# Even layer's value sums for two tiles of queries in one step, and the base weight block's copy moved from GpSimd to ScalarE

## The chip, the cores and the metric

The kernel runs on one NeuronCore of a Trainium2 chip. The metric is the device time of one execution in microseconds. The kernel before took 733.72 us (median of three runs, 733.67 to 733.96). The execution that the profiler recorded took 733.63 us; the span from its first to its last instruction is 731.9 us, so 1.7 us lie outside the span. All durations below come from that one execution.

## The reference

A two-layer encoder trunk on 256 tokens of width 1024, in float32. The even layer runs two kinds of attention side by side (8 heads of windowed two-dimensional attention with a bias, 8 heads of latent attention), the odd layer a mixture of three dilated windows. Each layer is followed by an MLP with a squared ReLU.

```python
for layer in range(DEPTH):                       # 2
    xn = rms_norm(x, norm_mix[layer])
    if layer % 2 == 0:
        x = x + even_mixer(xn, ...)              # softmax(q k^T + bias) v, two kinds
    else:
        x = x + odd_mixer(xn, ...)
    x = x + sq_relu_mlp(rms_norm(x, norm_mlp[layer]), mlp_w1[layer], mlp_w2[layer])
return rms_norm(x, norm_final)

def sq_relu_mlp(xn, w1, w2):                     # 1024 -> 4096 -> 1024
    return jnp.square(jax.nn.relu(xn @ w1)) @ w2
```

## The kernel before, in words

Every float32 weight is split on the chip into a high part (`whi`, a cast on ScalarE, line 205) and a low part (`wlo`, a subtraction on VectorE, line 206), and each product is three matmuls of these parts (`mm3`, lines 209 to 211). The whole weight set streams through the core once: `specs` lists the weight pieces in order of use, `load_weight` fetches a piece into one of four `raw` buffers by a DMA of the SyncE queue (line 151), `split_piece` splits it into one of three `whi`/`wlo` buffers, and `weight()` hands it to the matmuls, with loads four pieces ahead and splits two pieces ahead. So a cast waits until TensorE has let go of the piece three places back, and a load waits until the piece four places back has been split.

**Even layer.** `scores(n)` computes the scores and the softmax of one item (two heads, one tile of 128 queries), `turn_probs(n)` transposes the probabilities on TensorE (line 816) and copies them out, and `mix(n)` multiplies them with the values (four float32 matmuls, line 830, recorded as eight instructions) and splits the sum. There are 16 items. `attention()` lists these steps, and they are woven between the large projections.

**MLP.** Up pieces (U, from `w1`) and down pieces (D, from `w2`) alternate: U0 U1 U2 D0 U3 D1 and so on to D15. The down product uses seven block products in place of eight (`SEVEN`), for which sums of weight blocks are needed. For D0 to D13 of each MLP, `load_weight` does it in part by DMA: the base block goes into the first half of a `sum` buffer (three buffers; SyncE queue, line 143), **GpSimd copies it into the second half (line 144)**, and a DMA of GpSimd's queue adds two more blocks onto both halves while it writes (line 145). VectorE adds further blocks to that (`more_sums`, lines 179 and 180: these results go back into `raw` and into `every`), and `split_sums` splits the three sums into `sumh` (ScalarE) and `suml` (VectorE). Between these, the engines compute the hidden layer: ReLU and square on ScalarE (373, 375), three combinations on VectorE (380 to 382), their cast `hh` on ScalarE, and `hl` on VectorE.

Each engine executes its own instructions in the order that the program's scheduler has written; an instruction that waits holds up all behind it on that engine. The k-th line 179 needs what the k-th line 145 has added, and in VectorE's order it stands behind the splits of the sums before it (`suml`, `hl`) and ahead of the two low parts of the down piece before it.

Of the kernel before, what the change touches and what calls it, by code (L numbers as in the profile page):

```python
# [19 lines left out]
F32 = mybir.dt.float32  # L20
F32R = mybir.dt.float32r
AF = mybir.ActivationFunctionType
# [4 lines left out]
P = 128  # L27
D = 1024
KT = D // P
T = 256  # L30
NT = T // P
# [10 lines left out]
BLK = 512  # L42
LOAD_AHEAD = 4
# [6 lines left out]
def trunk(ctx, tc, a, out):  # L50
    nc = tc.nc
# [23 lines left out]
    def quarter_pair(name):  # L75
        return [act.tile([P, KT // 2, T], F32R, tag="quarter", name=name + v, bufs=4) for v in "hl"]

    def bank(tag):
        return ps.tile([P, 512], F32, tag=tag, name=tag)

    x = act.tile([P, KT, T], F32, name="x")
# [24 lines left out]
    specs = []  # L106
# [24 lines left out]
    plan_mlp(1)  # L131

    parts = {}
    state = {"loaded": 0, "split": (0, 0), "used": 0, "pool": None, "parts_done": None}

    def load_weight(pieces=1, before=lambda i: None):
        j = state["loaded"]
        src, n, _, seven = specs[j]
        if seven:

            blocks = src.rearrange("p (b n) -> p b n", n=BLK)
            sums = state["pool"].tile([P, 2, BLK], F32, tag="sum", name="sum", bufs=3)
            nc.sync.dma_start(sums[:, 0, :], blocks[:, 3, :])
            nc.gpsimd.tensor_copy(out=sums[:, 1, :], in_=sums[:, 0, :])  # L144
            nc.gpsimd.dma_start(sums, blocks[:, 0:3:2, :], accum_op=ALU.add)
            n = 3 * BLK
        raw = wraw.tile([P, WCH], F32, tag="raw", name="raw")
        for i in range(pieces):
            c = slice(i * n // pieces, (i + 1) * n // pieces)
            before(i)  # L150
            nc.sync.dma_start(raw[:, c], src[:, c])
        parts[j] = [raw, None, None] + ([sums] if seven else [])
        state["loaded"] = j + 1
# [5 lines left out]
    def split_piece(eng=None):  # L159
        j, i = state["split"]  # L160
        _, _, n, seven = specs[j]
        state["split"] = (j, i + 1) if i < n - (not seven) else (j + 1, 0)
        if i == 0:
            parts[j][1:3] = (wsp.tile([P, WCH], F32R, tag=v, name=v) for v in ("whi", "wlo"))
            if seven:

                with tc.issue_after(state["parts_done"]):
                    more_sums(parts[j])
        if i == n:
            parts[j][1:3] = split_sums(parts[j])  # L170
            return
        raw, hi, lo = (z[:, cut(j, i, n)] for z in parts[j][:3])
        return split(hi, lo, raw, eng)
# [16 lines left out]
    def prefetch(loads, splits):  # L190
        while state["loaded"] < min(loads, len(specs)):
            load_weight()
        while state["split"] < (min(splits, len(specs)), 0):
            split_piece()

    def weight():

        j = state["used"]
        prefetch(j + 1, j + 1)
        prefetch(j + LOAD_AHEAD, j + SPLIT_AHEAD)  # L200
        state["used"] = j + 1
        return parts.pop(j)[1:3]

    def split(hi, lo, src, eng=None):
        a = nc.scalar.copy(hi, src).ins  # L205
        return a, (eng or nc.vector).tensor_tensor(lo, src, hi.bitcast(F32), op=ALU.subtract).ins  # L206

    def mm3(o, sh, sl, mh, ml, first, last):
        nc.tensor.matmul(o, sh, mh, start=first, stop=False)  # L209
        nc.tensor.matmul(o, sh, ml, start=False, stop=False)  # L210
        nc.tensor.matmul(o, sl, mh, start=False, stop=last)  # L211

    def two_heads(o, hi, lo, ts):

        for n, (y, z) in enumerate(((hi, hi), (hi, lo), (lo, hi))):
            for j in range(2):
                pb = slice(64 * j, 64 * j + 64)
                nc.tensor.matmul(o[j], y[pb, 0, ts], z[pb, 1, :], start=n == 0, stop=n == 2)  # L218
# [10 lines left out]
    def tok(t):  # L229
        return slice(t * P, (t + 1) * P)  # L230
# [8 lines left out]
    def two(z):  # L239
        return z.rearrange("p (f n) -> p f n", f=2)  # L240
# [7 lines left out]
    def add_squares(b, s):  # L248

        q = scratch([2, T], "q") if b else two(s)  # L250
        nc.scalar.activation(q, x[:, 2 * b:2 * b + 2, :], AF.Square)
        if b:
            nc.vector.tensor_tensor(two(s), two(s), q, op=ALU.add)
        if b == 3:
            return nc.vector.tensor_tensor(s[:, 0:T], s[:, 0:T], s[:, T:2 * T], op=ALU.add).ins
# [308 lines left out]
    def even(ep):  # L564
# [208 lines left out]
        mixed = [quarter_pair("oa"), None]  # L773
        items = [(0, t, hp) for hp in range(4) for t in range(NT)] + [(1, t, hp) for hp in range(4) for t in range(NT)]
        biases, probs, turned = {}, {}, {}

        def load_bias(n):
            if n < 8:
                _, t, hp = items[n]
                biases[n] = ep.tile([P, 2, T], F32, tag="bias", name="bias", bufs=2)  # L780
                nc.sync.dma_start(biases[n], a["rpb"][t, hp])

        def scores(n):
            kind, t, hp = items[n]
            load_bias(n + 2)

            sb = [bank("w")[:, 0:T] for _ in range(2)] if kind == 0 else bank("w").rearrange("p (j n) -> p j n", j=2)
            s_of = lambda j: sb[j] if kind == 0 else sb[:, j]
            if kind == 0:
                two_heads(sb, *qk[hp], tok(t))  # L790
            else:
                for j in range(2):
                    h = 2 * hp + j
                    (qh, ql), (kh, kl) = mT["q"], mT["k"]
                    mm3(sb[:, j], qh[0:96, h, tok(t)], ql[0:96, h, tok(t)], kh[0:96, h, :], kl[0:96, h, :], True, True)
            pp, sn = scratch([2, T], "pp"), scratch([2, T], "sn")
            mn, z, rz = (work.tile([P, 2], F32, tag=v, name=v, bufs=3) for v in ("mn", "z", "rz"))
            for j in range(2):
                o = s_of(j)
                if kind == 0:  # L800
                    nc.vector.tensor_tensor_reduce(out=sn[:, j], in0=o, in1=biases[n][:, j, :], op0=ALU.add, op1=ALU.min,
                                                   scale=-1.0, scalar=3e38, accum_out=mn[:, j:j + 1])
                else:
                    nc.vector.tensor_scalar(sn[:, j], o, -MLA_SCALE, None, ALU.mult, ALU.min, accum_out=mn[:, j:j + 1])
            for j in range(2):
                nc.scalar.activation(pp[:, j], sn[:, j], AF.Exp, bias=mn[:, j:j + 1], scale=-1.0, accum_out=z[:, j:j + 1])
            nc.vector.reciprocal(rz, z)
            for j in range(2):
                nc.scalar.activation(pp[:, j], pp[:, j], AF.Copy, scale=rz[:, j:j + 1])
            probs[n] = pp  # L810
# [7 lines left out]
            nc.any.tensor_copy(out=turned[n], in_=pt.rearrange("p (b n) -> p b n", b=4))  # L818

        def mix(n):  # L820
            kind, t, hp = items[n]
            pts = turned.pop(n)
            if mixed[kind] is None:
                mixed[kind] = quarter_pair("ob")
            v = (vna, vml)[kind]
            pvo = bank("acc" if n < 6 else "w")
            for kk in range(NT):
                for j in range(2):
                    h = 2 * hp + j
                    nc.tensor.matmul(pvo[64 * j:64 * j + 64, 0:P], v[:, kk, h * 64:(h + 1) * 64], pts[:, 2 * j + kk, :],  # L830
                                     start=kk == 0, stop=kk == NT - 1)
            split(*(z[:, hp, tok(t)] for z in mixed[kind]), pvo[:, 0:P])

        def attention():

            out = []
            for n in range(len(items) + 2):
                for fn, m in ((scores, n), (turn_probs, n - 1), (mix, n - 2)):
                    if 0 <= m < len(items):
                        out.append(lambda fn=fn, m=m: fn(m))  # L840
                if n == 0:
                    out += [lambda: None] * 2
            return out
# [21 lines left out]
        main += [(0, lambda: accs.extend(open_accs()))]  # L865
        main += [(1.3, f) for k in range(6) for f in out_steps(accs, mixed, wo, k)]
        side = attention()
        at = -5
        total = sum(c for c, _ in main) + at
# [296 lines left out]
```

## Time and profile before

| what | value |
|---|---|
| profiled execution | 733.63 us |
| its span | 731.9 us |
| busy: VectorE, ScalarE, GpSimd | 623.0, 522.6, 78.8 us |
| granted TensorE clock, mean | 0.998 |
| even layer with its norm, from the first score matmul to the first MLP's norm sums | 39 to 133 us |
| first MLP: down pieces D0 to D13 | from 133 us, one down and one up piece every 10.54 us |
| second MLP: down pieces from D0 | from 570 us |

Rows of the timeline read: start in us, duration in us, engine, line, operation, result from operands, shape, count; in brackets the idle time of the engine before it and what ended it. Durations of neighbours on one engine overlap a little, so the cost of an instruction to its engine is the distance from its start to the next one's. PE is TensorE, PEld its weight loads, DVE VectorE, ACT ScalarE, POOL GpSimd, SPq the SyncE queue.

### The profile page before, as it was taken

Reading aid. Unit: us, or ns where it says so; the run is one execution under the profiler, and the core shown is the slowest. Engines: PE = TensorE matmul, PEld = TensorE weight load, DVE = VectorE, ACT = ScalarE, POOL = GpSimd, SP = SyncE. Lnnn points to the kernel's source line nnn. Section 1 sums busy time; section 2 is a strip of 40 time slices with the busy share of each in tenths; the row PEclk is TensorE's granted clock in tenths of the full one; section 3 lists DMA queues with packets and bytes.
Section 4 is the critical chain, followed back from the end, with each engine's and each line's share of the span. In section 5 each row is a group of like instructions: output and inputs, shape, how many; then the busy total and the mean of one; then the engine's idle time right before and its main releaser. Section 6 shows DMA issues by size and latency. Waiting matters only on the chain.

```text
span 731.9 us, 13834 instructions
## 1 busy us (share of the span) xinstructions
PE 723.1 (99%) x5234; PEld 660.6 (90%) x5234; DVE 623.0 (85%) x1188; ACT 522.6 (71%) x986; POOL 78.8 (11%) x73
## 2 busy tenths in 40 slices
PE   9999999999999999999999999999999999999996
PEld 6988899999999998989899899998999999999995
DVE  6888859999999959989777888778759998999956
ACT  7778968767767756878676767867658766766752
POOL 0100002224222000000000000000002422232000
PEclk9999999999999999999999999999999999999999
DMA  8773338798989644664655456455658798898611
GB/s 317 274 264 133 116 116 216 216 287 244 265 263 255 193 165 166 216 207 150 229 178 171 170 188 211 170 188 198 199 195 201 235 277 221 259 273 242 211 39 59
DMA packets 38499, 149.56 MB, mean 204 GB/s; under 512 B 5152, under 2 KB 7200, under 8 KB 29344
## 3 DMA queue, kind: packets, MB, share of 16 engines
q1 hardware_dynamic: 30384, 133.71, 52.0%
q0 software_dynamic: 7616, 14.68, 12.0%
q8 instruction: 41, 0.67, 0.4%
q10 hardware_dynamic: 432, 0.28, 0.1%
q14 instruction: 26, 0.21, 0.1%
HBM read 142.10 MB, written 1.05 MB: 196 GB/s over the span
## 4 chain that ended last, share of the span: by engine, by line
PE 83%; issue 10%; DVE 3%; DMA 2%; ACT 1%; POOL 0%; SPq 0%; POOLq 0%; DVEq 0%; ACTq 0%
PE acc L937 11%; PE acc L209 10%; PE w L209 10%; PE w L210 10%; PE w L211 10%; PE acc L210 10%; PE acc L211 9%; PE acc L938 5%; PE w L218 1%; PE w L1014 1%; DMA sum<-in_w 1%; PE acc L1029 1%; PE w L816 1%; PE w L830 1%; DMA raw<-in_w_cv 1%
## 5 line engine op out<-in xcount | busy, mean ns | idle before, releaser
L206 DVE TENSOR_TENSOR wlo<-raw,whi 128x512 fp32r<-128x512 f32 (+3 forms) x360 | 296.7, 845 | 51.3 <-ACT whi L205 51.1
L205 ACT CAST whi<-raw 128x512 fp32r<-128x512 f32 (+3 forms) x360 | 253.6, 746 | 86.7 <-PE w L210 59.0
L210 PE MATMUL w<-xx,whi 128*128 128x256 f32 x528 | 149.6, 283 | 0.0
L211 PE MATMUL w<-xx,wlo 128*128 128x256 f32 x528 | 149.3, 283 | 0.0
L209 PE MATMUL w<-xx,whi 128*128 128x256 f32 x528 | 148.9, 283 | 0.0
L937 PE MATMUL acc<-xx,whi 128*128 128x512 f32 x336 | 122.0, 404 | 0.0
L210 PEld LDWEIGHTS w<-xx,whi 128*128 128x128 f32 x528 | 101.2, 192 | 1.5 <-DVE xx L246 0.4
L209 PEld LDWEIGHTS w<-xx,whi 128*128 128x128 f32 x528 | 101.0, 192 | 1.1
L211 PEld LDWEIGHTS w<-xx,wlo 128*128 128x128 f32 x528 | 101.2, 192 | 0.0
L938 PE MATMUL acc<-xx,wlo 128*128 128x256 f32 x336 | 94.3, 281 | 0.0
L144 POOL COPY sum<-sum 128x512 f32<-128x512 f32 x28 | 42.2, 1523 | 461.6 <-DVE wlo L206 279.2
L937 PEld LDWEIGHTS acc<-xx,whi 128*128 128x128 f32 x336 | 63.1, 188 | 14.1
L938 PEld LDWEIGHTS acc<-xx,wlo 128*128 128x128 f32 x336 | 63.5, 189 | 0.0
L209 PE MATMUL acc<-whi,xx 128*128 128x384 f32 (+2 forms) x160 | 55.6, 350 | 0.0
L210 PE MATMUL acc<-wlo,xx 128*128 128x384 f32 (+2 forms) x160 | 55.2, 345 | 0.1
L211 PE MATMUL acc<-whi,xx 128*128 128x384 f32 (+2 forms) x160 | 54.7, 342 | 0.0
L205 ACT CAST hh<-h 128x896 fp32r<-128x896 f32 (+1 forms) x32 | 28.9, 904 | 24.2 <-DVE h L382 23.2
L209 PE MATMUL w<-whi,hh 128*128 128x512 f32 (+1 forms) x108 | 42.1, 390 | 0.0
L210 PE MATMUL w<-wlo,hh 128*128 128x512 f32 (+1 forms) x108 | 41.5, 384 | 0.0
L211 PE MATMUL w<-whi,hl 128*128 128x512 f32 (+1 forms) x108 | 41.2, 382 | 0.0
L206 DVE TENSOR_TENSOR hl<-h,hh 128x896 fp32r<-128x896 f32 (+1 forms) x32 | 35.6, 1112 | 0.0
L206 DVE TENSOR_TENSOR suml<-sum,sumh 128x1024 fp32r<-128x1024 f32 x28 | 34.0, 1214 | 0.0
(234 smaller groups left out, 1544.4 us busy)
## 6 DMA issues: line engine op xcount, KB each, us to landing
raw<-in_w SPq DMA_DIRECT2D x36, 1024.0 KB, 5.1
raw<-in_w_oqk SPq DMA_DIRECT2D x24, 1024.0 KB, 4.9
raw<-in_w SPq DMA_DIRECT2D x28, 768.0 KB, 4.9
sum<-in_w POOLq DMA_DIRECT2D x28, 512.0 KB, 7.8
raw<-in_w_ov SPq DMA_DIRECT2D x16, 768.0 KB, 4.4
sum<-in_w SPq DMA_DIRECT2D x28, 256.0 KB, 5.7
sw<-qk SPq DMA_DIRECT2D x84, 64.0 KB, 2.6
raw<-in_w_oe SPq DMA_DIRECT2D x4, 1024.0 KB, 6.1
```

The costliest lines, as they stand in the source:

```text
L144: nc.gpsimd.tensor_copy(out=sums[:, 1, :], in_=sums[:, 0, :])
L205: a = nc.scalar.copy(hi, src).ins
L206: return a, (eng or nc.vector).tensor_tensor(lo, src, hi.bitcast(F32), op=ALU.subtract).ins
L209: nc.tensor.matmul(o, sh, mh, start=first, stop=False)
L210: nc.tensor.matmul(o, sh, ml, start=False, stop=False)
L211: nc.tensor.matmul(o, sl, mh, start=False, stop=last)
L218: nc.tensor.matmul(o[j], y[pb, 0, ts], z[pb, 1, :], start=n == 0, stop=n == 2)
L816: nc.tensor.transpose(pt[:, b * P:(b + 1) * P], pp[:, b // 2, (b % 2) * P:(b % 2 + 1) * P], ident)
L830: nc.tensor.matmul(pvo[64 * j:64 * j + 64, 0:P], v[:, kk, h * 64:(h + 1) * 64], pts[:, 2 * j + kk, :], start=kk == 0, stop=kk == NT - 1)
L937: nc.tensor.matmul(two(pq), wh[:, ws], xT[:, k], start=k == 0, stop=False)
L938: nc.tensor.matmul(pq[:, T:2 * T], wl[:, ws], xh[:, k, :], start=False, stop=k == KT - 1)
L1014: nc.tensor.transpose(pt[:, b * P:(b + 1) * P], pp[:, at:at + P], ident)
```

## The change

Three edits. (1) `mix` is run once for both tiles of queries of two heads: eight matmuls into one bank and one split of 256 columns, in place of twice four matmuls and a split of 128. The steps are listed in another order (`scores(n)` and, at odd n, the mix of the pair as one step; the transposition as the next), and the softmax's exponential writes over its own input (`pp = sn`). (2) The base block's load is a function of its own, `load_base`, called from `weight()` for the piece one place beyond the load distance; where it was called early, the copy of the base block runs on ScalarE, placed behind the last cast issued before it (`last_hi`). (3) The first D of each MLP keeps the copy on GpSimd.

```diff
+    bases = {}
+    def load_base(j):
+        sums = state["pool"].tile([P, 2, BLK], F32, tag="sum", name="sum", bufs=3)
+        nc.sync.dma_start(sums[:, 0, :], specs[j][0][:, 3 * BLK:4 * BLK])
+        bases[j] = sums
     def load_weight(pieces=1, before=lambda i: None):
...
-            sums = state["pool"].tile([P, 2, BLK], F32, tag="sum", name="sum", bufs=3)
-            nc.sync.dma_start(sums[:, 0, :], blocks[:, 3, :])
-            nc.gpsimd.tensor_copy(out=sums[:, 1, :], in_=sums[:, 0, :])
+            early = j in bases
+            if not early:
+                load_base(j)
+            sums = bases.pop(j)
+            if early:
+                with tc.issue_after(state["last_hi"]):
+                    nc.scalar.copy(sums[:, 1, :], sums[:, 0, :])
+            else:
+                nc.gpsimd.tensor_copy(out=sums[:, 1, :], in_=sums[:, 0, :])
             nc.gpsimd.dma_start(sums, blocks[:, 0:3:2, :], accum_op=ALU.add)
...
         prefetch(j + 1, j + 1)
+        ahead = j + LOAD_AHEAD + 1
+        if ahead < len(specs) and specs[ahead][3] and specs[j][0].tensor.name in ("in_w1", "in_w2"):
+            load_base(ahead)
         prefetch(j + LOAD_AHEAD, j + SPLIT_AHEAD)
...
     def split(hi, lo, src, eng=None):
-        a = nc.scalar.copy(hi, src).ins
+        a = state["last_hi"] = nc.scalar.copy(hi, src).ins
...
-            pp, sn = scratch([2, T], "pp"), scratch([2, T], "sn")
+            pp = sn = scratch([2, T], "pp")
...
         def mix(n):
-            kind, t, hp = items[n]
-            pts = turned.pop(n)
+            kind, _, hp = items[n]
...
-            for kk in range(NT):
-                for j in range(2):
-                    h = 2 * hp + j
-                    nc.tensor.matmul(pvo[64 * j:64 * j + 64, 0:P], v[:, kk, h * 64:(h + 1) * 64], pts[:, 2 * j + kk, :], ...)
-            split(*(z[:, hp, tok(t)] for z in mixed[kind]), pvo[:, 0:P])
+            for t in range(NT):
+                pts = turned.pop(n - 1 + t)
+                for kk in range(NT):
+                    for j in range(2):
+                        h = 2 * hp + j
+                        nc.tensor.matmul(pvo[64 * j:64 * j + 64, tok(t)], v[:, kk, h * 64:(h + 1) * 64], pts[:, 2 * j + kk, :], ...)
+            split(*(z[:, hp, :] for z in mixed[kind]), pvo[:, 0:T])
...
-                for fn, m in ((scores, n), (turn_probs, n - 1), (mix, n - 2)):
-                    if 0 <= m < len(items):
-                        out.append(lambda fn=fn, m=m: fn(m))
+                now = [(scores, n)] + [(mix, n - 2)] * (n % 2 and n > 2)
+                for step in (now, [(turn_probs, n - 1)]):
+                    step = [(fn, m) for fn, m in step if 0 <= m < len(items)]
+                    if step:
+                        out.append(lambda step=step: [fn(m) for fn, m in step])
```

What this does to the order of the instructions shows at three places. The first is TensorE in the even layer. Before, a value product of one item (line 830, four matmuls) stands alone between the projection's matmuls and the next scores (line 218):

```order
L210 MATMUL acc<-xx,whi 128x256
L211 MATMUL acc<-xx,wlo 128x256
L830 MATMUL acc<-pts,vna 64x128 x4
L218 MATMUL w<-qk_h 128x256 x2
L218 MATMUL w<-qk_l,qk_h 128x256 x2
```

In the changed kernel (lines moved by 17 to 19: 226 to 228 are `mm3`, 235 the scores, 849 the value product), two items' products stand together:

```order
L235 MATMUL w<-qk_h 128x256 x2
L235 MATMUL w<-qk_l,qk_h 128x256 x2
L235 MATMUL w<-qk_h,qk_l 128x256 x2
L849 MATMUL acc<-pts,vna 64x128 x8
L226 MATMUL acc<-xx,whi 128x256
```

Over the whole program the value products of the even layer stand in 17 unbroken groups before (one item's is cut in two) and in 12 after: five pairs stay whole, and the other three pairs are cut by other matmuls into two or three groups.

The second place is ScalarE in the first MLP, around the eleventh `sumh<-sum`. Before:

```order
L375 ACTIVATE h<-relu 128x2x2x128
L205 CAST whi<-raw 128x1024 x2
L205 CAST sumh<-sum 128x1024
L205 CAST sumh<-every 128x512
L205 CAST hh<-h 128x896
```

After (line 222 is the cast, 392 the square, 156 the new copy):

```order
L392 ACTIVATE h<-relu 128x2x2x128
L222 CAST whi<-raw 128x1024 x2
L156 COPY sum<-sum 128x512
L222 CAST sumh<-sum 128x1024
L222 CAST sumh<-every 128x512
L222 CAST hh<-h 128x896
```

The copy stands between the second pair of casts and the k-th `sumh`. It is the copy for the sum after that one: the first copy stays on GpSimd, so ScalarE's k-th copy serves the accumulating DMA number k+1. In the second MLP three of the copies, the seventh, ninth and eleventh, stand one place later, behind `hh`:

```order
L222 CAST whi<-raw 128x1024 x2
L222 CAST hh<-h 128x896
L156 COPY sum<-sum 128x512
L222 CAST sumh<-sum 128x1024
L222 CAST sumh<-every 128x512
```

The third place is GpSimd. Before, copies and accumulating DMAs alternate:

```order
L144 COPY sum<-sum 128x512
L145 DMA sum<-in_w 128x2x512
L144 COPY sum<-sum 128x512
L145 DMA sum<-in_w 128x2x512
L144 COPY sum<-sum 128x512
L145 DMA sum<-in_w 128x2x512
```

After, each MLP keeps one copy there, and the other accumulating DMAs follow one another (286 and 253 are the norms' powers):

```order
L158 COPY sum<-sum 128x512
L159 DMA sum<-in_w 128x2x512 x14
L286 TENSOR_TENSOR rstd<-ms,mhalf 128x2
L158 COPY sum<-sum 128x512
L159 DMA sum<-in_w 128x2x512 x14
L253 TENSOR_TENSOR rstd<-ss,mhalf 128x1 x2
```

On the SyncE queue the sequence of base blocks and `raw` pieces is the same in both kernels from the eighth down piece of each MLP on; the scheduler had placed the base block's load one cycle ahead before, too. On VectorE the order in the MLPs is nearly unchanged.

More of the change, by code (lines that the diff above doesn't have):

```diff
@@ L133, in trunk @@
     parts = {}
-    state = {"loaded": 0, "split": (0, 0), "used": 0, "pool": None, "parts_done": None}
+    state = {"loaded": 0, "split": (0, 0), "used": 0, "pool": None, "parts_done": None, "last_hi": None}
+    bases = {}
[3 more added lines that the diff above has]
+        bases[j] = sums
     def load_weight(pieces=1, before=lambda i: None):
@@ L250, in add_squares @@
         q = scratch([2, T], "q") if b else two(s)
-        nc.scalar.activation(q, x[:, 2 * b:2 * b + 2, :], AF.Square)
+        state["last_hi"] = nc.scalar.activation(q, x[:, 2 * b:2 * b + 2, :], AF.Square).ins
         if b:
@@ L826, in mix @@
             pvo = bank("acc" if n < 6 else "w")
-            for kk in range(NT):
-                for j in range(2):
-                    h = 2 * hp + j
-                    nc.tensor.matmul(pvo[64 * j:64 * j + 64, 0:P], v[:, kk, h * 64:(h + 1) * 64], pts[:, 2 * j + kk, :],
-                                     start=kk == 0, stop=kk == NT - 1)
-            split(*(z[:, hp, tok(t)] for z in mixed[kind]), pvo[:, 0:P])
+            for t in range(NT):
[3 more added lines that the diff above has]
+                        h = 2 * hp + j
+                        nc.tensor.matmul(pvo[64 * j:64 * j + 64, tok(t)], v[:, kk, h * 64:(h + 1) * 64], pts[:, 2 * j + kk, :],
+                                         start=kk == 0, stop=kk == NT - 1)
+            split(*(z[:, hp, :] for z in mixed[kind]), pvo[:, 0:T])
         def attention():
```

## Prediction

> **What bounds the kernel now.** I read the page first (busy times, chain), then the waits by engine, then the timeline of one even-layer stretch and of one cycle in each MLP.
>
> ```profile
> span 731.9 us, 13834 instructions
> PE 723.1 (99%) x5234; PEld 660.6 (90%) x5234; DVE 623.0 (85%) x1188; ACT 522.6 (71%) x986; POOL 78.8 (11%) x73
> PE 83%; issue 10%; DVE 3%; DMA 2%; ACT 1%; POOL 0%; SPq 0%; POOLq 0%; DVEq 0%; ACTq 0%
> PE acc L90 <- DVE warm L85: 1.2, 1, 1.2
> PE w L287 <- DVE diag L280: 0.2, 1, 0.2
> ```
>
> TensorE is busy for 99% of the span and carries the chain. Its longest recorded wait is 1.2 us at the very start; the next is 0.2 us. So the time is TensorE's stream of matmuls plus start and tail, which the change does not touch. Two things can move it: a shorter stream, or a new wait in it. An engine that is only relieved gains nothing.
>
> **The even layer: a shorter stream.** Two columns matter, the starts and the counts.
>
> ```profile
> 52.34 0.28 PE L209 MATMUL acc<-xx,whi 128*128 128x256 f32 x1
> 52.45 0.28 PE L210 MATMUL acc<-xx,whi 128*128 128x256 f32 x1
> 52.58 0.28 PE L211 MATMUL acc<-xx,wlo 128*128 128x256 f32 x1
> 52.78 0.66 PE L830 MATMUL acc<-pts,vna 128*64 128x128 f32 x8
> 53.37 0.38 PE L218 MATMUL w<-qk_h 64*128 64x256 f32 x2
> 53.59 0.28 PE L218 MATMUL w<-qk_l,qk_h 64*128 64x256 f32 x2
> ```
>
> Projection matmuls start 0.12 us apart. The last one before the value product holds 0.20, the value product 0.59 (52.78 to 53.37), and the first score row 0.22 where such a row inside a run holds 0.12. Within the group the eighth instruction starts at 0.66 - 0.27 = 0.39 (0.27 is the length of one such matmul), so 0.055 each, 0.44 for eight. The group costs 0.08 + 0.59 + 0.10 = 0.77, of which 0.33 is paid for entering and leaving. The order shows 17 groups before and 12 after: 5 x 0.33 = **1.7 us less**. Bounds: nothing, if the trace's step at a group's edge only moves to the transpositions beside it; 3.0, if a pair that is cut by other matmuls costs no more than a whole one (8 groups, 9 x 0.33). I take 1.7, since the same work stays and only edges go. Eight casts and eight subtractions fewer on ScalarE and VectorE are hidden behind this stream, and so is the softmax written in place.
>
> **The MLPs: the copy's new place.** One cycle (a down and an up piece) of the first MLP:
>
> ```profile
> 213.29 0.80 POOL L144 COPY sum<-sum 128x512 f32<-128x512 f32 x1 [9.58 <-DMA sum<-in_w]
> 214.40 1.09 POOL L145 DMA_DIRECT2D sum<-in_w  x1 [0.30 <-POOL sum L144]
> 216.91 0.68 DVE L179 TENSOR_TENSOR raw<-sum,raw 128x512 f32<-128x512 f32 x1
> 218.69 1.23 DVE L206 TENSOR_TENSOR wlo<-raw,whi 128x1024 fp32r<-128x1024 f32 x1 [0.37 <-ACT whi L205]
> 220.12 1.23 DVE L206 TENSOR_TENSOR wlo<-raw,whi 128x1024 fp32r<-128x1024 f32 x1 [0.21 <-ACT whi L205]
> 222.74 0.29 DVE L381 TENSOR_TENSOR h<-h 128x128 f32<-128x128 f32 x1
> 224.07 0.70 DVE L382 TENSOR_TENSOR h<-h 128x128 f32<-128x128 f32 x1
> 227.45 0.68 DVE L179 TENSOR_TENSOR raw<-sum,raw 128x512 f32<-128x512 f32 x1
> 217.61 1.05 ACT L205 CAST whi<-raw 128x1024 fp32r<-128x1024 f32 x1 [2.34 <-PE w L210]
> 220.52 1.99 ACT L205 CAST whi<-raw 128x1024 fp32r<-128x1024 f32 x2
> 223.51 0.62 ACT L205 CAST sumh<-every 128x512 fp32r<-128x512 f32 x1
> 224.86 0.95 ACT L205 CAST hh<-h 128x896 fp32r<-128x896 f32 x1 [0.73 <-DVE h L382]
> 217.53 0.40 PE L209 MATMUL w<-whi,hh 128*128 128x512 f32 x1
> 228.07 0.40 PE L209 MATMUL w<-whi,hh 128*128 128x512 f32 x1
> ```
>
> How long an accumulating DMA takes from its issue to its landing (in the first MLP, in the second, in a calm stretch, in the busiest), and what a copy of 512 columns costs ScalarE, taken from its square of the same size:
>
> ```profile
> sum<-in_w POOLq DMA_DIRECT2D x14, 512.0 KB, 9.1
> sum<-in_w POOLq DMA_DIRECT2D x14, 512.0 KB, 7.4
> sum<-in_w POOLq DMA_DIRECT2D x1, 512.0 KB, 6.2
> sum<-in_w POOLq DMA_DIRECT2D x6, 512.0 KB, 9.9
> L251 ACT ACTIVATE q<-x 128x512 f32<-128x512 f32 x12 | 6.9, 619 | 0.0
> ```
>
> GpSimd copied as soon as the base block had landed (213.29). The DMA issued at 214.40 is the twelfth, and the twelfth line 179 is the one at 227.45: 13.05 us for a landing of 9.1, so 3.9 us to spare. In the changed order the copy for that sum stands on ScalarE behind the pair of casts that ends at 222.51. Then: 222.51 + 0.62 (copy) + 0.30 (copy to issue) = 223.4, landing at 232.5. Line 179 is next on VectorE at 227.45 and waits **5.1 us**, and all of VectorE's cycle behind it: the two low parts of the down piece, the hidden layer's combinations, the sums. The first of those low parts is done at 219.92 and used by TensorE at 228.07, so 8.1 us of lateness are hidden. One late cycle costs nothing.
>
> But lateness feeds back: line 382 late makes `hh` late, `hh` stands ahead of the next casts on ScalarE, and behind those casts stands the next copy but one. The circle takes: copy 0.62, to issue 0.30, landing L, from line 179 to the end of line 382 216.91 to 224.77 = 7.86 less 0.58 idle and less 0.41 (line 382 took 0.70 beside GpSimd's copy, line 381, of the same size, 0.29) = 6.87, hand-over 0.09, `hh` 0.95, casts 217.61 to 222.51 = 4.90, and 0.2 for two more hand-overs: 13.93 + L. It spans two cycles, 2 x 10.54 = 21.08. With L = 9.1 it lacks 1.95 us each time. ScalarE's copies 4 to 13 make four such rounds: 7.8. First MLP: 5.1 + 7.8 - 8.1 = **4.8 us** of waiting on TensorE. The circle closes without loss below L = 7.15.
>
> The second MLP, where every second copy stands behind `hh` from the seventh to the eleventh:
>
> ```profile
> 648.11 1.99 ACT L205 CAST whi<-raw 128x1024 fp32r<-128x1024 f32 x2
> 661.01 0.95 ACT L205 CAST hh<-h 128x896 fp32r<-128x896 f32 x1
> 655.87 0.68 DVE L179 TENSOR_TENSOR raw<-sum,raw 128x512 f32<-128x512 f32 x1
> 660.53 0.29 DVE L382 TENSOR_TENSOR h<-h 128x128 f32<-128x128 f32 x1
> 665.75 0.68 DVE L179 TENSOR_TENSOR raw<-sum,raw 128x512 f32<-128x512 f32 x1
> 634.08 0.40 PE L209 MATMUL w<-whi,hh 128*128 128x512 f32 x1
> 655.65 0.40 PE L209 MATMUL w<-whi,hh 128*128 128x512 f32 x1
> 649.81 3.14 SPq L151 DMA_DIRECT2D raw<-in_w  x2
> ```
>
> Here L was 7.4, but the copy moves to the moment at which two `raw` pieces are issued (649.81 beside casts that end at 650.10), so I take 8.2, half-way to the first MLP's 9.1. From one copy to the next: 0.62 + 0.30 + 8.2 + 4.95 (655.87 to 660.82) less 0.3 for the stretch beside GpSimd + 0.09 + 0.95 + 0.2 = 15.0. From 650.1 the copy behind `hh` starts at 665.1 in place of 661.96; its sum lands at 665.1 + 0.92 + 8.2 = 674.2 for a line 179 at 665.75: 8.5 late. From there to the next copy 0.62 + 1.62 (two sum casts, 222.51 to the end of the second, 224.13) + 4.90 = 7.1, so two cycles take 22.1 against 21.57 (634.08 to 655.65): 0.5 twice. 8.5 + 1.0 - 8.1 = **1.4 us**.
>
> Costed at nothing: GpSimd's 26 copies (GpSimd is the bound nowhere); 26 x 0.62 = 16 us on ScalarE, which waits 2.34 us for TensorE in each cycle; the earlier call for base blocks, since their order on the SyncE queue hardly changes. Were ScalarE's cover gone, the copies would be paid in full, 16 us.
>
> **Sum:** 733.63 - 1.7 + 4.8 + 1.4 = **738.1 us**, against a profiled execution 0.1 below the median of the runs.
>
> Two rules, weighed:
>
> ```profile
> L145 POOL DMA_DIRECT2D sum<-in_w x28: 1083/1087/1689, 109.4 to 672.7; - x28
> ```
>
> All but a few of the 28 issues took GpSimd the same 1.09 us, whatever VectorE did beside them. The Trainium skill, page "SBUF — State Buffer", section "Who interferes with whom", says that only VectorE and GpSimd share a port pair, as a lock, and that ScalarE waits for nobody; by it the stretch of 0.41 that I took off goes with the copy, and the trace agrees for the copy (0.70 beside 0.29). Were the stretch to stay, by descriptor writing in place of the copy, four rounds of each MLP would grow by 0.4 and the sum by about 3 us, to 741. The Trainium skill, page "DMA: Bandwidth & Descriptors", section "Issuing engines are not separate DMA queues", says that transfers of all queues share the same 16 engines; by it the accumulations stay as slow as the `raw` loads beside them make them, which speaks for L near 9.
>
> **Rivals.** (a) *The accumulations land sooner*, not slower than before: the circle costs nothing if L stays under about 7. Of the rows, 6.2 speaks for it, 9.1 and 9.9 against it; a cycle that is stretched also leaves the DMA engines more room. At 6.2 the first MLP's line 179 is 2.2 us late, its circle takes 20.1 of 21.08, the second MLP's lateness stays under 8.1, and only the even layer counts: 733.63 - 1.7 = **731.9**. It decides from L = 7.15 in the first MLP. (b) *The busy stretch's 9.9 holds in both*: first MLP 5.9 + 4 x 2.75 - 8.1 = 8.8; second: copy 4.9 late, its sum 11.9 late, 2.2 more in each of two rounds, 8.3. Sum 733.6 - 1.7 + 17.1 = **749**. (c) *The gain cancels the waits*: L near 7.8 in the first MLP gives 3.8 + 4 x 0.65 - 8.1, nothing, and 1.4 in the second: **733.3**. (d) *The change does not do what it says*: the base loads come no earlier in steady state, as the order shows; that is in the sum already.
>
> **How the numbers follow.** Chances: forecast with its neighbours up to (b) 0.58, (b) and beyond 0.12, (c) 0.13, (a) 0.17. Range: from (a) with 0.3 more in the even layer, **731.6**, up to **748**, just short of (b); I leave 0.05 below and 0.08 above. A difference within 0.2% (1.5 us) is about what a measurement cannot tell from no change: faster 0.17, same 0.13, slower 0.70.
>
> **What would show it.** In the changed profile: even layer 1.7 us shorter, with eight-matmul groups at 1.2 us. VectorE's line 179 (now 193) waiting for the DMA of `sum`, several times by 1 to 5 us. TensorE waiting for `wlo` in the later half of each MLP, and cycles over 10.54 us. GpSimd's issues right behind ScalarE's copies. I am wrong if accumulations land within 7 us, or if VectorE's lateness stays under 8 us through both MLPs.

## The result

The changed kernel takes **763.2 us** (median of 4 runs, 760.56 to 763.65), the kernel before 733.84 us on the same chip; the ratio is 1.0392 with a 95% interval from 1.0368 to 1.0416. The forecast was slower, 738.1 us, with a range up to 748: the sign holds, the size is more than six times too small (29.4 us slower in place of 4.5). One run in this document, of e5's kernel below, was a slow one (1582.8 us at a mean granted clock of 0.45) and is left out.

The page of the changed kernel: span, busy times of the engines, and the shares of the chain that ended last.

```profile
span 761.6 us, 13799 instructions
PE 731.2 (96%) x5234; PEld 665.1 (87%) x5234; DVE 612.0 (80%) x1179; ACT 533.5 (70%) x1005; POOL 38.4 (5%) x47
PE 44%; issue 28%; DMA 13%; DVE 10%; ACT 3%; POOL 1%; SPq 0%; POOLq 0%; DVEq 0%; ACTq 0%
```

TensorE's share of the chain fell from 83% to 44%, and DMAs, which held 2%, hold 13%. The waits by engine (line, what it waited for: us in total, times, longest):

```profile
PE w L506 <- ACT relu L390: 7.7, 3, 4.0
PE acc L226 <- ACT whi L222: 6.3, 3, 3.2
PE w L226 <- ACT relu L390: 5.2, 5, 2.1
PE acc L227 <- DVE wlo L223: 1.8, 4, 0.8
PE w L227 <- DVE wlo L223: 1.0, 1, 1.0
DVE raw L193 <- DMA sum<-in_w: 55.5, 15, 6.8
ACT hh L222 <- DVE h L399: 55.3, 18, 5.0
```

Read from the bottom: VectorE's line 193 waits 55.5 us for accumulating DMAs, ScalarE's cast `hh` waits as long for VectorE, and TensorE waits 22 us, most of it for ScalarE, and only 2.8 for the low parts of VectorE.

Where the 29.7 us between the two spans lie shows in the starts of some matmuls on TensorE: the first matmul of the first and of the second down piece, and of the up piece behind it, in both MLPs (before, line 209 has them at 133.11, 143.75, 148.54, and at 569.79, 580.43, 585.22):

```profile
131.23 0.48 PE L226 MATMUL w<-whi,hh 128*128 128x512 f32 x1
141.87 0.40 PE L226 MATMUL w<-whi,hh 128*128 128x512 f32 x1
152.57 0.28 PE L226 MATMUL w<-xx,whi 128*128 128x256 f32 x1
580.51 0.48 PE L226 MATMUL w<-whi,hh 128*128 128x512 f32 x1
591.15 0.40 PE L226 MATMUL w<-whi,hh 128*128 128x512 f32 x1
602.72 0.28 PE L226 MATMUL w<-xx,whi 128*128 128x256 f32 x1
```

| stretch | before | after | difference |
|---|---|---|---|
| start to the first MLP's first down piece | 133.11 | 131.23 | -1.88 |
| from there to the second MLP's first down piece | 436.68 | 449.28 | +12.60 |
| of this, the second down piece | 4.79 | 10.70 | +5.91 |
| from there to the end of the span | 162.11 | 181.09 | +18.98 |
| of this, the second down piece | 4.79 | 11.57 | +6.78 |

The even layer gives what was forecast, and by the price that was put on it. A whole pair on TensorE (eight matmuls, recorded as sixteen instructions):

```profile
99.93 0.28 PE L228 MATMUL w<-kh,ql 96*128 96x256 f32 x1
100.14 1.09 PE L849 MATMUL w<-pts,vml 128*64 128x128 f32 x16
101.39 0.28 PE L227 MATMUL acc<-obl,whi 128*128 128x256 f32 x1
```

From 99.93 to 101.39 are 1.46 us, less 0.24 for the two other matmuls that start in this stretch: 1.22, where two single groups cost 2 x 0.77. That is 0.32 a pair, 1.6 for the five whole pairs. Each MLP then loses in two ways: at once in its second down piece, and over the later cycles (6.7 and 12.2 us).

**The start.** ScalarE, GpSimd, VectorE and TensorE around the first MLP's second down piece, of the kernel before GpSimd alone:

```profile
115.31 2.20 POOL L145 DMA_DIRECT2D sum<-in_w  x2
```

and after:

```profile
129.40 0.61 ACT L156 COPY sum<-sum 128x512 f32<-128x512 f32 x1
130.32 1.09 POOL L159 DMA_DIRECT2D sum<-in_w  x1 [17.27 <-ACT sum L156]
136.76 0.69 DVE L193 TENSOR_TENSOR raw<-sum,raw 128x512 f32<-128x512 f32 x1 [2.30 <-DMA sum<-in_w]
142.52 1.99 ACT L222 CAST sumh<-sum 128x1024 fp32r<-128x1024 f32 x2 [5.20 <-DMA sum<-in_w]
146.35 0.50 PE L226 MATMUL acc<-whi,hh 128*128 128x512 f32 x1 [2.93 <-ACT whi L222]
```

Before, GpSimd copied the second base block as soon as it had landed and issued the second and third accumulation one behind the other, from 115.31; now the second is issued at 130.32 and the third at 134.15. Here it is not VectorE that passes the lateness on: the casts of the sums on ScalarE (142.52) wait for the DMA themselves, for 5.20 us, and the high parts of the down piece that TensorE is about to need stand behind them.

**The later cycles, first MLP.** One round of the circle:

```profile
207.32 0.61 ACT L156 COPY sum<-sum 128x512 f32<-128x512 f32 x1
208.24 1.09 POOL L159 DMA_DIRECT2D sum<-in_w  x1 [11.42 <-DVE wlo L223]
217.78 0.69 DVE L193 TENSOR_TENSOR raw<-sum,raw 128x512 f32<-128x512 f32 x1 [4.07 <-DMA sum<-in_w]
224.57 0.95 ACT L222 CAST hh<-h 128x896 fp32r<-128x896 f32 x1 [4.72 <-DVE h L399]
226.38 0.58 ACT L390 ACTIVATE relu<-w 128x512 f32<-128x512 f32 x1
227.01 0.39 PE L226 MATMUL w<-xx,whi 128*128 128x256 f32 x1 [0.51 <-ACT relu L390]
230.22 0.61 ACT L156 COPY sum<-sum 128x512 f32<-128x512 f32 x1
```

The copy at 207.32 leads to an issue at 208.24 and a landing 9.5 us later, for which line 193 has waited 4.07 us; `hh` follows 6.79 us after it, and the next copy but one 5.65 us after that. Round trip 22.90 us; the prediction's 13.93 + L with this L of 9.54 is 23.47. But the place where TensorE feels it is another one: the ReLU stands behind `hh` and a cast, and TensorE cannot start the next up piece in the same bank before it is done.

**The second MLP.** The same circle, longer where the copy stands behind `hh`:

```profile
639.54 0.62 ACT L156 COPY sum<-sum 128x512 f32<-128x512 f32 x1
640.46 1.09 POOL L159 DMA_DIRECT2D sum<-in_w  x1 [14.07 <-ACT sum L156]
650.36 0.69 DVE L193 TENSOR_TENSOR raw<-sum,raw 128x512 f32<-128x512 f32 x1 [6.75 <-DMA sum<-in_w]
657.15 0.94 ACT L222 CAST hh<-h 128x896 fp32r<-128x896 f32 x1 [4.71 <-DVE h L399]
659.58 0.77 PE L506 MATMUL w<-ident,x 128*128 128x128 f32 x4 [4.03 <-ACT relu L390]
664.48 0.94 ACT L222 CAST hh<-h 128x896 fp32r<-128x896 f32 x1 [0.81 <-DVE h L399]
665.32 0.62 ACT L156 COPY sum<-sum 128x512 f32<-128x512 f32 x1
```

Issue 0.92 us after the copy, line 193 another 9.90 us later; from there VectorE works without a gap over 0.2 us, through its part of this cycle and of the next, and the `hh` of the *next* cycle starts 14.12 us behind line 193; the copy stands 0.84 behind that. Round trip 25.78 us where two cycles took 21.57.

**The clock.** Stretches of time: length, busy time of TensorE (matmuls, weight loads), VectorE, ScalarE and GpSimd with their instructions, granted TensorE clock, DMA share, GB/s.

```profile
145.00:155.00 10.00, 7.84 (x36) 6.48 (x37) 9.61 (x14) 9.56 (x13) 1.09 (x1) 0.83 0.70 243
270.00:280.00 10.00, 7.94 (x48) 7.36 (x47) 8.73 (x10) 6.25 (x8) 0.00 (x0) 0.83 0.66 242
595.00:605.00 10.00, 8.62 (x35) 6.93 (x36) 9.37 (x13) 9.16 (x12) 1.09 (x1) 0.66 0.68 220
660.00:665.00 5.00, 5.00 (x20) 4.12 (x18) 4.90 (x8) 3.99 (x6) 0.00 (x0) 0.66 0.45 164
685.00:690.00 5.00, 4.92 (x30) 4.42 (x31) 4.61 (x8) 3.87 (x6) 0.00 (x0) 1.00 0.46 187
```

After four of its waits TensorE runs at a lower clock. What is missing to 1.00, times the length, is 1.7 + 1.7 + 3.4 + 1.7 = 8.5 us over the first four; this is an upper bound, since TensorE also stood waiting for some 1.2 us of the third stretch's low clock. With the 22 us of waits that is about 30 of the 31.6 us that the two MLPs lost.

### The profile page after: what moved, and what is told of

It is laid out like the page before. It is cut to its first block, busy times and chain, and to the rows that moved or that the text cites. A ratio compares the mean times of both kernels' runs of the same rounds, so it can differ in the third digit from the quotient of the medians.

```text
span 761.6 us, 13799 instructions
## 1 busy us (share of the span) xinstructions
PE 731.2 (96%) x5234; PEld 665.1 (87%) x5234; DVE 612.0 (80%) x1179; ACT 533.5 (70%) x1005; POOL 38.4 (5%) x47
## 4 chain that ended last, share of the span: by engine, by line
PE 44%; issue 28%; DMA 13%; DVE 10%; ACT 3%; POOL 1%; SPq 0%; POOLq 0%; DVEq 0%; ACTq 0%
DMA sum<-in_w 13%; PE acc L959 10%; PE acc L226 6%; PE acc L227 6%; PE acc L228 6%; PE acc L960 5%; DVE wlo L223 5%; PE w L235 1%; PE w L1036 1%; ACT whi L222 1%; PE acc L1051 1%; PE w L833 1%; DVE suml L223 1%; PE w L226 1%; PE w L227 1%
## 5 line engine op out<-in xcount | busy, mean ns | idle before, releaser
L193 DVE TENSOR_TENSOR raw<-sum,raw 128x512 f32<-128x512 f32 x28 | 19.3, 689 | 55.8 <-DMA sum<-in_w 55.5
L226 PE MATMUL acc<-whi,xx 128*128 128x384 f32 (+2 forms) x160 | 55.5, 349 | 0.2 <-ACT whi L222 0.2
L159 POOL DMA_DIRECT2D sum<-in_w x28 | 30.7, 1095 | 268.2 <-ACT sum L156 207.1
L222 ACT CAST sumh<-sum 128x1024 fp32r<-128x1024 f32 x28 | 29.2, 1049 | 18.6 <-DMA sum<-in_w 18.3
```

Of the source, the lines that this page charges most:

```text
L193: nc.vector.tensor_tensor(raw[:, 3, :], sums[:, 1, :], raw[:, 0, :], op=ALU.add)
L222: a = state["last_hi"] = nc.scalar.copy(hi, src).ins
```

## The experiments

Thirteen experiments on twelve kernels (e12 is e5's kernel once more). The times are medians, of e11 and e12 a single run; the kernel before took 733.7 to 733.8 us beside them.

**e1, the even layer's edit alone**, on the kernel before:

```diff
-            pp, sn = scratch([2, T], "pp"), scratch([2, T], "sn")
+            pp = sn = scratch([2, T], "pp")
...
-            kind, t, hp = items[n]
+            kind, _, hp = items[n]
...
+            for t in range(NT):
+                pts = turned.pop(n - 1 + t)
```

> The kernel before with the even layer's edit alone (value sums in pairs, pp = sn); base loads and copies as before. Theory (the loss is all in the MLPs, and the even layer gains what the first down piece's earlier start shows, 133.11 to 131.23 us): 733.8 - 1.9 = 731.9 us. Rival (the even layer's new order also disturbs what comes later, the loads ahead of the first MLP for one): over 735.

735.47 us, ratio 1.0023 (1.0012 to 1.0034): 0.2% slower, the rival's number. The first down piece does start early, at 131.32, but then GpSimd, VectorE and TensorE show this:

```profile
155.18 9.67 POOL L144 COPY sum<-sum 128x512 f32<-128x512 f32 x1 [10.15 <-DVE every L180]
171.82 0.69 DVE L179 TENSOR_TENSOR raw<-sum,raw 128x512 f32<-128x512 f32 x1 [7.46 <-issue]
181.14 0.38 PE L209 MATMUL w<-xx,whi 128*128 128x256 f32 x1 [2.57 <-ACT relu L373]
```

One copy on GpSimd, 0.80 us in the row of the prediction, takes 9.67 us, through a stretch in which VectorE runs one instruction after the other, and ends 0.48 us after VectorE's last instruction there, line 180 at 163.69, has ended. (Before, the longest such copy took 4.35 us.) The accumulation behind it is late, and TensorE waits 2.57 us for the ReLU; e13, the same kernel without this copy, does not lose the time. That the earlier entry into the MLP is what brings the copy into this stretch is likely, but no run shows it by itself.

**e2, the copy and base loads alone**, with the even layer as before (the hunks of e1 undone in the changed kernel):

> The changed kernel with the even layer as before: only the early base load and ScalarE's copy remain. Theory (all the loss is here): 763.2 + 1.9 = about 765 us, with VectorE waiting over 50 us for the accumulating DMAs. Rival (the two edits interact): under 755.

763.15 us, ratio 1.0401 (1.0378 to 1.0423): as much as the whole change, so all of the loss is here. VectorE waits 56.8 us for the sums. Whether the even layer's 1.9 us survive in the whole change cannot be read from these two: their runs scatter over 3 and 4 us.

**e3, the copy back on GpSimd**, all else as changed:

```diff
-                with tc.issue_after(state["last_hi"]):
-                    nc.scalar.copy(sums[:, 1, :], sums[:, 0, :])
+                nc.gpsimd.tensor_copy(out=sums[:, 1, :], in_=sums[:, 0, :])
```

> The changed kernel with the copy back on GpSimd; the early base load and the even layer stay. Theory (ScalarE's copy makes the accumulations late): 731.9 us, VectorE's line 193 waits under 5 us for the sums. Rival (the base loads that are called earlier collide with the raw loads): 745 to 763.

736.1 us, ratio 1.0031 (1.0021 to 1.0041): 27 us of the loss are gone with ScalarE's copy; the base loads that are called earlier are not its cause. What is left, 4 us over the theory, goes with the event of e1: here too one copy on GpSimd takes 9.94 us, VectorE waits once for 7.5 us, and TensorE for 2.6.

**e4, ScalarE's copy without its place:**

```diff
-                with tc.issue_after(state["last_hi"]):
-                    nc.scalar.copy(sums[:, 1, :], sums[:, 0, :])
+                nc.scalar.copy(sums[:, 1, :], sums[:, 0, :])
```

> The changed kernel without the placing behind the last cast: the scheduler now sets ScalarE's copy one cycle earlier (three sum casts follow the last copy of the first MLP, in place of two). Theory (only the moment of the copy counts, its work on ScalarE is hidden): 731.5 to 736 us. Rival (ScalarE's 16 us of added work, or its reads beside VectorE, cost the time): over 750.

734.31 us, ratio 1.0010 (0.9996 to 1.0023). The same 26 copies on the same engine, one cycle earlier, leave the time where it was before the change. One of them in the first MLP:

```profile
214.99 0.62 ACT L155 COPY sum<-sum 128x512 f32<-128x512 f32 x1 [2.03 <-DMA sum<-in_w]
```

Here ScalarE waits for the base block and not the reverse. So ScalarE's added work is hidden, as forecast, all but at most the 2.4 us by which this time lies over the 731.9 that the even layer's gain alone would give (TensorE has three waits of 0.5 to 0.8 us here); and the moment of the copy is the cause of the 29 us.

**e5 and e6, the start and the rest apart.** In e5 the copies for the second to fourth sum are free (set by the scheduler, as in e4) and the others placed as in the change; e6 is the converse (`nth` counts the sums of an MLP from nought):

```diff
-                with tc.issue_after(state["last_hi"]):
-                    nc.scalar.copy(sums[:, 1, :], sums[:, 0, :])
+                nth = sum(s[3] for s in specs[:j]) % 14
+                if nth > 3:
+                    with tc.issue_after(state["last_hi"]):
+                        nc.scalar.copy(sums[:, 1, :], sums[:, 0, :])
+                else:
+                    nc.scalar.copy(sums[:, 1, :], sums[:, 0, :])
```

> The changed kernel, but ScalarE's copies for the second to fourth sum of each MLP are not placed behind the last cast (the scheduler sets them early); the others are placed as in the change. Theory (two losses: the stall in the second down piece of each MLP, 5.9 and 6.3 us with the low clock behind it, and the circle later on): 763.2 - 12.2 = 751 us. Rival (one loss: without the first stall, the same lateness stalls TensorE a few cycles later): 758 to 763.

> The converse: only the copies for the second to fourth sum of each MLP are placed behind the last cast. Theory of two losses: 734.3 + 12.2 = about 746.5 us, the stall at the second down piece only. Rival (that stall is caught up, or is a part of the circle): under 738.

e5: 757.2 us (756.43 to 759.63), ratio 1.0327 (1.0306 to 1.0348); e6: 744.73 us, ratio 1.0151 (1.0136 to 1.0167). From e4's 734.3, the start alone costs 10.4 us and the rest alone 22.9: 33.3 together, where the change loses 28.9 against e4. e6 lies near the theory, e5 far above it and just short of its rival: there are two losses, but they overlap by some 4 us. e12 shows how. (The expectation's 6.3 us for the second MLP's start was low; the table has 6.78.)

**e7, single late copies**, the condition of e5 changed to `nth in (5, 8, 11)`: the sixth, ninth and twelfth sum, counted from one (the expectation counts from nought).

> Only the copies for the fifth, eighth and eleventh sum of each MLP are placed behind the last cast, with early ones between. Theory (a late sum costs nothing by itself as long as VectorE's lateness stays under what ReLU's place covers, some 5.5 us in the first MLP and 2.3 where transpositions stand in the down piece of the second; the loss comes from lateness that feeds back): 734 to 738 us. Rival (each late sum costs its share of the 19 us that the 20 later ones lose): 734.3 + 6 = 740 us.

743.18 us, ratio 1.0127 (1.0094 to 1.016), above both. Two of the six waits of VectorE that the late sums bring, and TensorE's wait behind each:

```profile
201.20 0.69 DVE L197 TENSOR_TENSOR raw<-sum,raw 128x512 f32<-128x512 f32 x1 [3.20 <-DMA sum<-in_w]
210.51 0.39 PE L230 MATMUL w<-xx,whi 128*128 128x256 f32 x1 [0.20 <-ACT relu L394]
609.44 0.69 DVE L197 TENSOR_TENSOR raw<-sum,raw 128x512 f32<-128x512 f32 x1 [5.91 <-DMA sum<-in_w]
618.66 0.97 PE L510 MATMUL w<-ident,x 128*128 128x128 f32 x4 [4.51 <-ACT relu L394]
```

In the first MLP VectorE waits 1.91, 3.20 and 3.19 us for the three late sums, and TensorE 0.20 in all: a single one is hidden there, and the circle is needed for a loss. In the second MLP a single late sum is enough. VectorE waits 5.91, 6.50 and 6.54 us, and TensorE 4.51, 0.59 and 1.78. The longest wait is that of transpositions (line 510), which want the ReLU's bank in the middle of the down piece; the second, of 0.59, stands before transpositions too.

**e8, `hh` behind the next ReLU on ScalarE**, in the changed kernel:

```diff
-            nc.scalar.activation(r, pu, AF.Relu)
+            ri = nc.scalar.activation(r, pu, AF.Relu).ins
+            while held:
+                with tc.issue_after(ri):
+                    split(*held.pop())
...
-                split(hh[:, 0:7, :], hl, h[:, 0:7, :])
+                held.append((hh[:, 0:7, :], hl, h[:, 0:7, :]))
```

> The changed kernel with the cast of the hidden layer (hh) behind the next ReLU on ScalarE, so that a late hh does not hold up the ReLU that TensorE waits for. Theory (the cover that decides is ReLU's place behind hh): TensorE's waits for relu, 12.9 us, fall to under 2; the second down pieces stall as before; waits for low parts appear in their place only beyond 8.1 us of lateness; 745 to 755 us. Rival (the low parts of the down piece are what TensorE waits for first, as in the prediction): no gain, 760 or more.

827.09 us, ratio 1.1267 (1.1248 to 1.1286). It does not answer its question: the square on ScalarE writes the one buffer `h` and now waits for `hl` on VectorE,

```profile
ACT h L396 <- DVE hl L223: 148.6, 22, 8.7
```

so that the edit put a longer circle in place of the one that it was to cut. It was not tried in another form, and what the ReLU's place alone costs stays open.

**e9 and e10, no copy at all:** SyncE loads the base block into both halves, in the changed kernel (e9) and in the kernel before (e10; the copy is dropped in both).

```diff
-            nc.sync.dma_start(sums[:, 0, :], blocks[:, 3, :])
-            nc.gpsimd.tensor_copy(out=sums[:, 1, :], in_=sums[:, 0, :])
+            for h in range(2):
+                nc.sync.dma_start(sums[:, h, :], blocks[:, 3, :])
```

> The changed kernel with no copy at all: SyncE loads the base block into both halves of the sum (256 KB more for each of 28 pieces). Theory (the accumulations need only start early; a copy on GpSimd can be held up by VectorE for up to 9.7 us, as in the run with the even layer's edit alone, and ScalarE's is late by its place): the even layer's 1.9 us are kept, 731.5 to 733 us, no wait of VectorE for sums over 3 us. Rival (7.3 MB more of loads delay raw loads and accumulations): 735 or more.

> The kernel before with the base block loaded into both halves and no copy; even layer as before. Theory (before, GpSimd's copy cost nothing on TensorE's path): 733.7 us, the same as before. Rival (the added loads cost time): 736 or more; rival (GpSimd's copies did cost time): under 732.5.

e9: 735.59 us, ratio 1.0025 (1.0016 to 1.0034), the rival's number, and VectorE's longest wait for a sum is 3.8 us; e10: 733.57 us, ratio 0.9997 (0.9988 to 1.0005), as expected. So GpSimd's copies cost nothing before, and the added loads cost nothing by themselves. e9 loses at the entry of each MLP: TensorE waits 1.2 us for the norm's `ms`, 0.5 for `hh` and 1.0 for `hl`, and its clock is 0.73 in the five microseconds around the last (570 to 575). e13, the same without the early calls for the base loads, does not lose it; so the loss hangs on the doubled loads being called early.

**e11, the late moment on GpSimd:** ScalarE writes one column at the copy's place, and GpSimd copies behind it.

```diff
-                    nc.scalar.copy(sums[:, 1, :], sums[:, 0, :])
+                    nc.scalar.copy(sums[:, 1, 0:1], sums[:, 0, 0:1])
+                nc.gpsimd.tensor_copy(out=sums[:, 1, :], in_=sums[:, 0, :])
```

> The changed kernel with ScalarE writing one column of the second half at the copy's place, and GpSimd copying all of it behind that; this puts 0.5 us per piece less work on ScalarE and keeps the late moment. Theory (the moment alone): as the change or worse, 760 to 780 us, since GpSimd's copy can also be held up by VectorE. Rival (ScalarE's added work): under 750.

769.5 us in a single run: the late moment without ScalarE's copy loses as much, and in the same places (TensorE waits 15.3 us for the ReLU and 7.2 for casts in the second down pieces; in the change 12.9 and 6.3). Early copies are harmless to within a few microseconds on ScalarE (e4) and on GpSimd (e3), late ones cost some 30 us on either: the moment, and not the engine, is the cause.

**e12, e5's kernel once more:**

> A second look at the kernel with early copies for the second to fourth sum, for an undisturbed profile. Expected: one time of 756 to 760 us; no wait of TensorE for casts in the second down pieces (5.9 and 6.3 us in the change), and more waiting for ReLU in the later cycles than the change's 12.9 us, since nothing has taken VectorE's lateness away before.

758.5 us. TensorE's waits:

```profile
PE w L510 <- ACT relu L394: 10.0, 3, 4.5
PE w L230 <- ACT relu L394: 7.3, 6, 2.2
```

As expected: none for casts in the second down pieces, and 17.3 us for the ReLU in place of 12.9. The first of these comes at

```profile
181.03 0.39 PE L230 MATMUL w<-xx,whi 128*128 128x256 f32 x1 [2.25 <-ACT relu L394]
```

where the change's first comes at 227.01: without the stall at the start, VectorE's lateness reaches TensorE four cycles sooner.

**e13, e1 without the copy**, the edit of e10 on top of e1:

> The kernel before with the even layer's edit, and the base block loaded into both halves, where GpSimd copied it; base loads not called earlier. Theory (in the run with the even layer's edit alone one GpSimd copy of 9.67 us, held up while VectorE ran without a gap, gave the gain back and more): without the copy 733.6 - 1.9 = 731.7 us, and no wait of TensorE over 0.5 us in the first MLP. Rival (the first MLP, entered earlier, loses the time in another way, as the run with two loads and early base loads did): 733.5 to 736 us.

**732.29 us**, ratio 0.9982 (0.9973 to 0.9991), near the theory. TensorE's longest wait in the MLPs is one of 0.7 us, in the second (line 489 for the ReLU). This keeps the even layer's gain, all but 0.5 us of it, and is the one version of the study that is faster than the kernel before, by 0.2%.

## Why the prediction was right in sign and wrong in size

- **The even layer: right.** Forecast -1.7, measured -1.88 at the first down piece, of which the five whole pairs give 1.6. That the gain would last was taken for granted; e1 shows that it can be lost right behind.
- **The mechanism in the MLPs: right.** The copy's place makes the accumulation late, line 193 waits, `hh` is late, and the next copy but one with it. e3, e4 and e11 show it from both sides. Its size in the first MLP came near, 4.8 us forecast and 6.7 lost in the later cycles (4.1 of waits, 1.7 by the low clock), but in part by luck: the cover of 8.1 us was too large, as the second point says, and the stall at the start, which the sum did not have, took away lateness that would have cost TensorE more later on (e12). The cost at nothing of ScalarE's 16 us was right to within 2.4 us (e4).
- **L: near in the first MLP, low in the second.** It was taken as 9.1 and 8.2. In the changed kernel the medians of all 14 sums are 7.3 and 7.9, but long and short landings alternate. The issues of the circle that stalls (185.20, 208.24, 231.13 and 253.06) took 9.7, 9.5, 8.5 and 11.0 us, those between them 6.4 to 6.7; in the second MLP every second one from 615.27 on took 8.6 to 9.9, those between 6.5 to 7.0. A copy feeds the next copy but one, so there are two circles, and the slower one counts: the median alone would have spoken for rival (a). With 9.9 the prediction's own sum has 8.3 us in the second MLP, in rival (b), in place of 1.4.
- **The step that failed first: "ScalarE's copies 4 to 13 make four such rounds".** It starts the sum in mid-stream. The first MLP's second and third accumulation had been issued from 115.31 on, long before they were wanted, and the change delays the second by 15 us; ScalarE's own sum casts wait for them, ahead of the casts that TensorE needs at once. No term of the sum had that: 5.91 + 6.78 us with the low clock behind the waits, and in e6, where only this is left, 10.4 us.
- **The second: "8.1 us of lateness are hidden".** That is the slack of the low parts (it was counted to 228.07, the matmul of the high part; the low part is first used at 228.30). The ReLU has less, and the rows were there. Before, in the first MLP and in the second:

```profile
222.32 0.28 PE L209 MATMUL w<-xx,whi 128*128 128x256 f32 x1
652.88 0.94 ACT L205 CAST hh<-h 128x896 fp32r<-128x896 f32 x1 [1.16 <-DVE h L382]
656.69 0.59 ACT L373 ACTIVATE relu<-w 128x512 f32<-128x512 f32 x1
657.73 0.60 PE L489 MATMUL w<-ident,x 128*128 128x128 f32 x4
```

  One cycle after 222.32 the next up piece starts, at 232.86; the ReLU takes 0.59 and may start at 232.27, and `hh` 1.81 before it (224.57 to 226.38 above), at 230.46: 5.6 us after its start at 224.86 in the prediction's row. In the second MLP the transpositions want the bank at 657.73, so by the same count `hh` may start at 655.33, 2.45 us after its 652.88. In the changed kernel 12.9 of TensorE's 22 us of waits are for the ReLU, against 2.8 for low parts. The runs support this cover by the releasers that they record; the run that was to move it (e8) did not answer, so that the size of the cover, 5.6 and 2.45 us, is an estimate from these rows.
- **The third, in the second MLP: "two cycles take 22.1".** Its round runs through the sum that follows the late one, and through the `hh` of that sum's cycle. The late sum itself, which the copy behind `hh` brings, has to pass the `hh` of its own cycle and that of the next, 14.12 us behind line 193, before the next copy behind `hh` can start: 25.78 us a round.
- **The fourth: every microsecond of waiting was counted once.** The low clock behind four of them adds up to 8.5 us, part of it in the start's 5.91 and 6.78.

Rival (b) put a larger L in the same sum and came to 749; no rival had the start, the ReLU or the clock. (The 741 us for a stretch that stays counts four rounds in each MLP, where the sum itself has two in the second.)

## What to carry to other kernels

When an instruction moves to an engine with a long queue, its new neighbours decide, not its duration: here 26 copies of 0.62 us each left the kernel at 734.3 us one cycle earlier and brought it to 763.2 behind the last cast. Follow a delay from the first cycle on, where buffers that were filled early give slack that the steady state does not show, and follow it through every consumer on the engine that it holds up: the one with the least slack may be a neighbour in the queue, as the ReLU behind `hh`. And count more than the waits where an engine that never waited begins to: here up to 8.5 us of lower clock came on top of 22 us of waits.

## What the runs showed of the hardware

- **The clock.** Waits of 2.93 + 0.81 us (before the matmuls at 146.35 and 147.67), of 3.16 + 0.52 us (before 595.86 and 597.18) and of 4.03 us (before 659.58) were each followed by a lower granted clock (0.83 and 0.66 over ten us, 0.66 over five); so was one of 2.06 us (before 273.56, with 0.96 some 7 us earlier), while one of 2.15 us (before 685.08) was not, as the last row of the stretches shows. The Trainium skill, page "TensorE: Matmul & The Clock Gate", section "Part 1: The HAM clock gate (the "warmup" mystery)", says that an idle window of about 3.4 us halves the clock, that the window runs freely, and that a busy one brings it back. The trace agrees behind the long waits, where 512 columns start 0.43 us apart (598.20, 598.62, 599.05) in place of 0.23 (656.12 to 656.35 before), and where the clock comes back: microsecond by microsecond from 660 on it is 0.50, 0.50, 0.50, 0.80 and 1.00, so the drop lasted 3.4 us, as did those from 148 and from 274; the one from 595 lasted twice that. A wait thus cost 1.7 us of clock, 3.4, or none. The wait of 2.06 us that came before one of the drops is shorter than the page's idle window.
- **GpSimd beside VectorE.** The copy of 9.67 us in e1 against 0.80. The Trainium skill, page "SBUF — State Buffer", section "Who interferes with whom", says that VectorE with two inputs in SBUF contends with GpSimd's reads over a pair of ports, and, of the modes in which VectorE takes both ports, that who comes first holds them for the whole instruction. The trace agrees as far as times can show it, and goes further: the copy lasted through a whole run of VectorE's instructions, not one of 1.2 us, and in e1 as in e3 (9.94 us) it ended 0.48 us after that run.
